# Sliding-window attention on TensorE: both head groups of a query block in one pass, and two sample chains in place of four

## The chip, the cores and the metric

The kernel runs on one core of one Trainium2 chip. The metric is the device time of one execution in microseconds (us); the median of three runs is given. One further execution was taken by the hardware profiler; all lines of the profile come from it. Engines are named as the profile names them: PE is TensorE's matmuls, PEld its weight loads, DVE is VectorE, ACT is ScalarE, POOL is GpSimd, SP the queue that issues DMAs.

## The reference

A two-layer decoder step for 512 prompt tokens and 64 sample tokens (8 sequences of 8) that share the weights. Layer 0 is a Conformer convolution (width 31) beside sliding-window attention, layer 1 a Mamba-2 mixer; each layer ends with a convolutional feed-forward network. The part that the change touches is the attention of layer 0:

```python
def sink_attention(q, k, v, q_pos, k_pos, sinks):
    b, n, tq, h, d = q.shape            # d = 64
    kv = k.shape[3]                     # 2 key/value heads
    g = h // kv                         # 4 query heads on each
    qg = q.reshape(b, n, tq, kv, g, d)
    s = jnp.einsum('bnqkgd,bnskd->bnkgqs', qg, k).astype(jnp.float32) * (d ** -0.5)
    ...                                 # window mask of 128 keys, a learned sink in each head's softmax
    o = jnp.einsum('bnkgqs,bnskd->bnqkgd', p, v)
```

The prompt's 512 queries are four blocks of 128; a block sees its own 128 keys and the 128 before it (block 0 only its own). The samples see a cache of 128 keys for each sequence, and their own 8. Everything is fp32.

## The kernel before

Activations lie with channels on the 128 partitions and the 576 tokens along the free dimension. A dense product (`mm3`, L152) takes each weight and each activation as a sum of a high and a low part and issues three matmuls (L158 to L160), 288 tokens wide; `wh` (ACT, L148) and `wl` (DVE, L149) are the parts of a weight tile. `units` runs one projection tile after another, `out_proj` an output projection.

`mix0` is layer 0's mixer. After the projections that need all of TensorE come, from L509 on, three kinds of work that are put between each other:

- The last two value projections of the convolution branch, `val_unit(1)` and `val_unit(3)`: 48 dense matmuls each.
- The depthwise convolution. Three of its four channel tiles are done by DVE, one tap an instruction (`ca`, L683). The fourth (tile 1) is done by PE: `pe_conv(k0, k1)` issues, for each tap, three matmuls of 512 columns with a diagonal matrix (`dg`, L524 to L526) and a narrow one (`df`, L529). ACT makes the diagonals, three instructions a tap (L522, L522, L528). `dg` has four buffers, two taps' worth.
- The attention. The query tiles `qf[j]` hold head j of the first key/value head on partitions 0 to 63 and head j + 4 on partitions 64 to 127; `kf` holds the two key heads in the same way. `kv` (0 or 1) is the head group. `scores(n, kv)` issues four matmuls for query block n, each with the 64 rows of its group (`sc`, L581; 256 columns wide, 128 for block 0), and calls `softmax`: on DVE a masked maximum for each head (L555), three tiny operations (L557 to L559), on ACT an exponential for each head (L562), on DVE two tiny operations and a scaling for each head (L563 to L566). `values(n, kv)` issues, for each 128-key chunk, four transposes into a bank (`pt`, L598), a copy by ACT (`ptb`, L600), and one matmul of 512 columns into the 64 partitions of its group in `po` (L602). After both groups ACT copies `po` to `of`, four instructions (L608).

The loop at L612 is a pipeline of eight steps: `scores` of a step, then filler (a value projection in the first two, five or six convolution taps after), then `values` of the step before. The score tiles `sc` (two heads a tile) take turns in three PSUM banks, `pt` in two, `po` has one.

The samples' attention (L634 to L658) is four chains, one for each half of the sequences (bh) and head group (kv): four small score matmuls in 32-column strips (`sc<-kct`, L640), one against the new keys (L642), a `softmax` of one tile, two transposes (L647, L648), two copies (L650, L651), then one matmul for the new values (L653) and four for the cached ones (L655).

Then come the high and low parts of the attention's output (`oh`, `ol`, L168 and L169), the mean over channels for the LayerNorm of the convolution (`pm`, L691, needs all four `ca`), the squares (`csq`) and the output projection of the attention (`out_proj` at L701, the first L158 that reads `oh`).

A scheduler places the instructions of each engine's queue. It keeps the results' dependences but not the order of the source; within its queue an engine issues in order.

Of the kernel before, what the change touches and what calls it, by code (L numbers as in the profile page):

```python
# [8 lines left out]
AF = mybir.ActivationFunctionType  # L9
# [3 lines left out]
P = 128  # L13
NP = 512
# [34 lines left out]
class Builder:  # L49
# [300 lines left out]
    def mix0(self):  # L350
        nc, d = self.nc, self.d
# [193 lines left out]
        def softmax(scores, masks, scl, sinks, nsinks, width):  # L545

            n = len(scores)
            mx, den = self.Z("mx", 4, bufs=4), self.Z("den", 4, bufs=4)
            neg, es = self.Z("neg", 4, bufs=4), self.Z("es", 4, bufs=4)
            sm, held = [], []  # L550
            for i, s in enumerate(scores):
                if i % 2 == 0:
                    held.append(self.S("sm", NP))
                t = held[-1][:, (i % 2) * 256:(i % 2) * 256 + width]
                nc.vector.tensor_tensor_reduce(t, s, masks, 1.0, -3.0e38, op0=ADD, op1=MAX, accum_out=mx[:, i:i + 1])  # L555
                sm.append(t)
            nc.vector.scalar_tensor_tensor(neg[:, :n], mx[:, :n], -1.0, scl, op0=MUL, op1=MUL)  # L557
            nc.vector.tensor_tensor(neg[:, :n], neg[:, :n], nsinks, op=MIN)
            nc.vector.tensor_tensor(es[:, :n], neg[:, :n], sinks, op=ADD)  # L559
            nc.scalar.activation(es[:, :n], es[:, :n], AF.Exp)  # L560
            for i, t in enumerate(sm):
                nc.scalar.activation(t, t, AF.Exp, bias=neg[:, i:i + 1], scale=scl[:, i:i + 1], accum_out=den[:, i:i + 1])  # L562
            nc.vector.tensor_tensor(den[:, :n], den[:, :n], es[:, :n], op=ADD)  # L563
            nc.vector.reciprocal(den[:, :n], den[:, :n])
            for i, t in enumerate(sm):
                nc.vector.tensor_scalar(t, t, den[:, i:i + 1], None, op0=MUL)  # L566
            return sm, held


        pos = {}  # L570

        def scores(n, kv):
            rows = slice(kv * 64, kv * 64 + 64)
            k0 = max(n - 1, 0) * P
            width = (n + 1) * P - k0
            sc = []
            for j in range(4):
                if j % 2 == 0:
                    p = self.ps("sc", "sc")
                o = p[:, (j % 2) * width:(j % 2 + 1) * width]  # L580
                nc.tensor.matmul(o, qf[j][rows, n * P:(n + 1) * P], kf[rows, k0:k0 + width], start=True, stop=True)  # L581
                sc.append(o)
            c0 = n * 8 + kv * 4
            return softmax(sc, self.cv("amask", 256 - width, width), rsq[:, c0:c0 + 4],
                           self.pv("sink_p", kv * 4, 4), nsink[:, kv * 4:kv * 4 + 4], width)

        def values(n, kv, probs):
            pr, held = probs
            rows = slice(kv * 64, kv * 64 + 64)
            if kv == 0:  # L590
                pos[n] = self.ps("po", "po")
            po = pos[n]
            k0 = max(n - 1, 0)
            nch = n + 1 - k0
            for c in range(nch):
                pt = self.ps("pt", "pt")
                for j in range(4):
                    nc.tensor.transpose(pt[:, j * P:(j + 1) * P], pr[j][:, c * P:(c + 1) * P], self.ident)  # L598
# [3 lines left out]
                nc.tensor.matmul(po[rows, :], vt[:, ch * P + kv * 64:ch * P + kv * 64 + 64], ptb,  # L602
                                 start=c == 0, stop=c == nch - 1)
                self.free(ptb)
            self.free(held)
            if kv == 1:
                for j in range(4):
                    nc.scalar.activation(of[j][:, n * P:(n + 1) * P], po[:, j * P:(j + 1) * P], AF.Copy)  # L608

        todo = [(n, kv) for n in range(4) for kv in range(2)]  # L610
# [12 lines left out]
        (n, kv), pr = ready.pop(0)  # L623
        values(n, kv, pr)

        kct = [self.S("kct", 512) for _ in range(2)]
        vc = [self.S("vc", 512) for _ in range(2)]
        for i in range(2):
# [2 lines left out]
            nc.sync.dma_start(d["wk_old"][i], kct[i].rearrange("p (b s) -> p b s", s=P)[:, :, 8:])  # L631
            nc.sync.dma_start(d["wv_old"][i], vc[i][8:, :])
        po = self.ps("po", "po")
        for bh in range(2):  # L634
            for kv in range(2):
                rows = slice(kv * 64, kv * 64 + 64)
                p = self.ps("sc", "sc")
                for b4 in range(4):
                    b = bh * 4 + b4
                    nc.tensor.matmul(p[b4 * 32:b4 * 32 + 32, 0:P], qs[rows, b * 32:b * 32 + 32],  # L640
                                     kct[bh][rows, b4 * P:(b4 + 1) * P], start=True, stop=True)
                nc.tensor.matmul(p[:, P:192], qs[rows, bh * P:(bh + 1) * P], kf[rows, NP:], start=True, stop=True)  # L642
                c0 = 32 + bh * 2 + kv
                (pr,), held = softmax([p[:, 0:192]], self.cv("smask", bh * 192, 192), rsq[:, c0:c0 + 1],
                              self.pv("sink_s", kv), nsink[:, 8 + kv:9 + kv], 192)
                pt = self.ps("pt", "pt")
                nc.tensor.transpose(pt[:, 0:P], pr[:, 0:P], self.ident)  # L647
                nc.tensor.transpose(pt[0:64, P:2 * P], pr[:, P:192], self.ident)  # L648
                ptb = self.S("ptb", NP)
                nc.scalar.activation(ptb[:, 0:P], pt[:, 0:P], AF.Copy)  # L650
                nc.scalar.activation(ptb[0:64, P:2 * P], pt[0:64, P:2 * P], AF.Copy)  # L651
                o = po[rows, bh * P:(bh + 1) * P]
                nc.tensor.matmul(o, vts[0:64, kv * 64:kv * 64 + 64], ptb[0:64, P:2 * P], start=True, stop=False)  # L653
                for b4 in range(4):
                    nc.tensor.matmul(o[:, b4 * 32:b4 * 32 + 32],  # L655
                                     vc[bh][:, b4 * P + kv * 64:b4 * P + kv * 64 + 64],
                                     ptb[:, b4 * 32:b4 * 32 + 32], start=False, stop=b4 == 3)
                self.free(held, ptb)  # L658
# [608 lines left out]
```

## Time and profile before

| | us |
|---|---|
| median of 3 runs | 1622.1 (1620.45 to 1622.54) |
| the profiled execution | 1617.26 |
| its span in the profile | 1615.5 |
| PE busy in the span | 1588.7 (98%) |
| first score matmul, from the span's start | 100.98 |
| first matmul of the attention's output projection | 196.31 |

The page divides the span into busy times, 40 slices and groups of instructions. A timeline row gives the start, how long the row lasts, the engine, the line, what it writes and reads, the array's rows and columns in use, the shape and the number of instructions; in square brackets, how long the engine had been idle before it and who released it. An fp32 matmul is recorded as two instructions, a transpose as one. Rows of pipelined matmuls overlap, so what a stretch takes is read from the start of its row to the start of the next.

### The profile page before, as it was taken

The page shows a single profiled execution, that of the slowest core. Times are in us where ns is not written, and L with a number is a line of the kernel's source. Part 1 is how long each engine was busy: PE and PEld are TensorE (multiplying, and loading weights), DVE is VectorE, ACT ScalarE, POOL GpSimd, SP SyncE. Part 2 cuts the span into 40 slices and gives each one's busy share as a digit, 9 for nine tenths or more (in the row PEclk, how much of TensorE's full clock was granted, in tenths as well). Part 3 has the DMA queues.
Part 4 walks back from the last instruction along what each step waited for, and adds up shares of the span by engine and source line. Part 5 has one row for each costly group of instructions (what it writes and reads, how often), then busy time and mean ns, then how long its engine had stood idle before and what let it go on. Part 6 is the DMA issues. An engine that isn't in the chain of part 4 may idle for free.

```text
span 1615.5 us, 28735 instructions
## 1 busy us (share of the span) xinstructions
PE 1588.7 (98%) x11704; PEld 1504.8 (93%) x11704; DVE 1026.3 (64%) x1847; ACT 696.5 (43%) x1333; POOL 109.4 (7%) x322
## 2 busy tenths in 40 slices
PE   8999999999999999999999999999899999999999
PEld 8996699999999999998997998998799999999999
DVE  7898677654365355578796676676776653554552
ACT  7248654322122122378766556557352221221220
POOL 0000001000000000010301101101110000000000
PEclk9999999999999999999999999999899999999999
DMA  7222022222222222224335325234222222222222
GB/s 229 71 73 69 1 66 90 80 91 79 80 90 70 93 87 76 83 72 141 132 82 166 102 70 176 92 97 156 97 69 89 91 80 79 92 71 87 92 80 76
DMA packets 63633, 150.05 MB, mean 93 GB/s; under 512 B 18558, under 2 KB 19582, under 8 KB 63502
## 3 DMA queue, kind: packets, MB, share of 16 engines
q1 hardware_dynamic: 63502, 148.23, 28.8%
q8 instruction: 92, 1.51, 0.4%
q14 instruction: 39, 0.32, 0.1%
HBM read 133.86 MB, written 14.34 MB: 92 GB/s over the span
## 4 chain that ended last, share of the span: by engine, by line
PE 89%; DVE 5%; ACT 4%; DMA 2%; issue 1%; POOL 0%; SPq 0%; DVEq 0%; ACTq 0%
PE mm L158 25%; PE mm L160 25%; PE mm L159 25%; DVE cconv L734 1%; DMA acb<-acd 1%; PE yp L974 1%; ACT wh L148 1%; PE pst L923 1%; PE po L602 1%; PE sc L581 1%; PE pt L180 1%; PE pyo L987 1%; PE yp L972 1%; PE mm L524 1%; PE pr L191 1%
## 5 line engine op out<-in xcount | busy, mean ns | idle before, releaser
L158 PE MATMUL mm<-hh,wh 128*128 128x288 f32 (+1 forms) x2288 | 680.6, 298 | 8.4 <-ACT wh L148 7.7
L160 PE MATMUL mm<-hh,wl 128*128 128x288 f32 x2288 | 679.8, 297 | 0.1
L159 PE MATMUL mm<-hl,wh 128*128 128x288 f32 (+1 forms) x2288 | 677.9, 297 | 0.0
L148 ACT ACTIVATE wh<-wr 128x1024 fp32r<-128x1024 f32 (+1 forms) x215 | 223.4, 1039 | 544.1 <-issue 283.3
L158 PEld LDWEIGHTS mm<-hh,wh 128*128 128x128 f32 (+1 forms) x2288 | 429.6, 188 | 14.8 <-ACT wh L148 8.0
L160 PEld LDWEIGHTS mm<-hh,wl 128*128 128x128 f32 x2288 | 429.7, 188 | 4.6 <-issue 2.8
L159 PEld LDWEIGHTS mm<-hl,wh 128*128 128x128 f32 (+1 forms) x2288 | 429.8, 188 | 3.5 <-issue 1.4
L149 DVE TENSOR_TENSOR wl<-wr,wh 128x1024 fp32r<-128x1024 f32 (+1 forms) x215 | 257.7, 1199 | 78.3 <-ACT wh L148 78.1
L158 PE MATMUL mm<-yh,wh 128*128 128x288 f32 x960 | 286.8, 300 | 2.5 <-ACT yh L168 2.5
L159 PE MATMUL mm<-yl,wh 128*128 128x288 f32 x960 | 287.6, 300 | 0.0
L160 PE MATMUL mm<-yh,wl 128*128 128x288 f32 x960 | 286.1, 299 | 0.0
L158 PEld LDWEIGHTS mm<-yh,wh 128*128 128x128 f32 x960 | 182.1, 190 | 6.9 <-issue 3.3
L159 PEld LDWEIGHTS mm<-yl,wh 128*128 128x128 f32 x960 | 182.1, 190 | 4.4 <-issue 3.2
L160 PEld LDWEIGHTS mm<-yh,wl 128*128 128x128 f32 x960 | 181.8, 190 | 2.9 <-issue 2.8
L257 DVE TENSOR_TENSOR x<-x,mm 128x288 f32<-128x288 f32 x192 | 85.7, 451 | 154.8 <-PE mm L160 154.4
L302 DVE TENSOR_TENSOR gbuf<-mm,rs 128x224 f32<-128x224 f32 x44 | 17.2, 392 | 108.0 <-PE mm L160 108.0
L313 ACT ACTIVATE gsilu<-gconv,par 128x512 f32<-128x512 f32 x44 | 31.8, 724 | 115.1 <-DVE gconv L310 115.1
L310 DVE SCALAR_TENSOR_TENSOR gconv<-gbuf,par,gconv 128x592 f32<-128x592 f32 x88 | 73.1, 831 | 1.5
L323 DVE TENSOR_TENSOR gsilu<-mm,gsilu 128x288 f32<-128x288 f32 x88 | 40.0, 455 | 50.3 <-PE mm L160 50.3
L683 DVE SCALAR_TENSOR_TENSOR ca<-seg,par,ca 128x576 f32<-128x576 f32 x90 | 71.3, 810 | 0.3
L734 DVE SCALAR_TENSOR_TENSOR cconv<-cbuf,par,cconv 128x600 f32<-128x600 f32 x72 | 61.4, 856 | 11.6 <-ACT cconv L732 10.6
L955 ACT ACTIVATE ew<-acb,ac 128x128 f32<-128x128 f32 x128 | 41.2, 390 | 37.4 <-DMA acb<-acd 17.6
(315 smaller groups left out, 1735.0 us busy)
## 6 DMA issues: line engine op xcount, KB each, us to landing
wr<-in_w_gate SPq DMA_DIRECT2D x44, 512.0 KB, 3.3
wr<-in_w_up SPq DMA_DIRECT2D x44, 512.0 KB, 3.3
wr<-in_w_in_o SPq DMA_DIRECT2D x40, 512.0 KB, 3.4
wr<-in_w_down SPq DMA_DIRECT2D x32, 448.0 KB, 3.3
wr<-in_w_down SPq DMA_DIRECT2D x16, 512.0 KB, 3.5
acb<-acd SPq DMA_DIRECT2D x32, 256.0 KB, 3.5
h<-in_h SPq DMA_DIRECT2D x32, 256.0 KB, 2.9
out_ssm_s<-h SPq DMA_DIRECT2D x32, 256.0 KB, 2.4
```

The costliest lines, as they stand in the source:

```text
L148: nc.scalar.activation(hi[:, :n], raw[:, :n], AF.Copy)
L149: nc.vector.tensor_tensor(lo[:, :n], raw[:, :n], hi[:, :n].bitcast(F32), op=SUB)
L158: nc.tensor.matmul(out, hi[:, ws], xh[:, sl], start=i == 0, stop=False)
L159: nc.tensor.matmul(out, hi[:, ws], xl[:, sl], start=False, stop=False)
L160: nc.tensor.matmul(out, lo[:, ws], xh[:, sl], start=False, stop=i == n - 1)
L257: nc.vector.tensor_tensor(self.x[m][:, sl], self.x[m][:, sl], p[:, :HB], op=ADD)
L310: nc.vector.scalar_tensor_tensor(cv[:, :592], g[:, k:592 + k], w(k), cv[:, :592], op0=MUL, op1=ADD)
L313: nc.scalar.activation(sl[:, :NP], cv[:, :NP], AF.Silu, bias=b)
L323: nc.vector.tensor_tensor(sl[:, HALF[half]], p[:, :HB], sl[:, HALF[half]], op=MUL)
L683: nc.vector.scalar_tensor_tensor(a, sv[:, :, k:k + 8], w, a, op0=MUL, op1=ADD)
L734: nc.vector.scalar_tensor_tensor(cv[:, :600], g[:, k:600 + k], w(k), cv[:, :600], op0=MUL, op1=ADD)
L955: nc.scalar.activation(ew[:, cs], acb[:, cs], AF.Relu, bias=ac[:, o:o + 1], scale=-1.0)
```

## The change

`scores` and `values` take both head groups of a block at once, and `softmax` handles eight heads in place of four. The score matmuls are issued alternately for rows 0 to 63 and 64 to 127, each group into tiles of its own; a block now has four `sc` tiles, still in three banks. In `values`, both groups' transposes and copies come first, and the two matmuls into `po` follow each other, group 1 first; a hint keeps the second in its place. The loop has four steps, each with more taps (7 or 8), and the last taps stand before the last `values`. The samples' chains become one for each bh: both groups' scores, one `softmax` of two tiles, four transposes into one bank, two copies, and the value matmuls alternately for the two column halves. The scores of both bh now precede both value parts.

```diff
-        def scores(n, kv):
-            rows = slice(kv * 64, kv * 64 + 64)
+        def scores(n):
...
-            sc = []
+            sc = [None] * 8
             for j in range(4):
                 if j % 2 == 0:
-                    p = self.ps("sc", "sc")
-                o = p[:, (j % 2) * width:(j % 2 + 1) * width]
-                nc.tensor.matmul(o, qf[j][rows, n * P:(n + 1) * P], kf[rows, k0:k0 + width], start=True, stop=True)
-                sc.append(o)
...
+                    p = [self.ps("sc", "sc") for _ in range(2)]
+                for kv in range(2):
+                    rows = slice(kv * 64, kv * 64 + 64)
+                    o = sc[kv * 4 + j] = p[kv][:, (j % 2) * width:(j % 2 + 1) * width]
+                    nc.tensor.matmul(o, qf[j][rows, n * P:(n + 1) * P], kf[rows, k0:k0 + width], start=True, stop=True)
+            return softmax(sc, self.cv("amask", 256 - width, width), rsq[:, n * 8:n * 8 + 8],
+                           self.pv("sink_p", 0, 8), nsink[:, 0:8], width, (0, 1, 4, 5, 2, 3, 6, 7))
...
             for c in range(nch):
-                pt = self.ps("pt", "pt")
-                for j in range(4):
-                    nc.tensor.transpose(pt[:, j * P:(j + 1) * P], pr[j][:, c * P:(c + 1) * P], self.ident)
-                ptb = self.S("ptb", NP)
-                nc.scalar.activation(ptb, pt, AF.Copy)
+                ptb = []
+                for kv in range(2):
+                    pt = self.ps("pt", "pt")
+                    for j in range(4):
+                        nc.tensor.transpose(pt[:, j * P:(j + 1) * P], pr[kv * 4 + j][:, c * P:(c + 1) * P], self.ident)
+                    ptb.append(self.S("ptb", NP))
+                    nc.scalar.activation(ptb[-1], pt, AF.Copy)
                 ch = k0 + c
-                nc.tensor.matmul(po[rows, :], vt[:, ch * P + kv * 64:ch * P + kv * 64 + 64], ptb,
-                                 start=c == 0, stop=c == nch - 1)
+                for kv in (1, 0):
+                    m = nc.tensor.matmul(po[kv * 64:kv * 64 + 64, :], vt[:, ch * P + kv * 64:ch * P + kv * 64 + 64], ptb[kv],
+                                         start=c == 0, stop=c == nch - 1)
+                    if kv == 0:
+                        self.tc.keep_in_program_order(m)
...
-        for t_, it in enumerate(todo):
-            ready.append((it, scores(*it)))
-            if t_ in (0, 1):
-                self.units([val_unit((1, 3)[t_])], 1)
-                if t_:
-                    self.norm_end()
+        for n in range(4):
+            ready.append((n, scores(n)))
+            if n == 0:
+                self.units([val_unit(1), val_unit(3)], 1)
+                self.norm_end()
             else:
-                pe_conv((t_ - 2) * 31 // 6, (t_ - 1) * 31 // 6)
+                pe_conv((n - 1) * 31 // 4, n * 31 // 4)
             if len(ready) > 1:
-                (n, kv), pr = ready.pop(0)
-                values(n, kv, pr)
-        (n, kv), pr = ready.pop(0)
-        values(n, kv, pr)
+                values(*ready.pop(0))
+        pe_conv(3 * 31 // 4, 31)
+        values(*ready.pop(0))
...
+            for b4 in range(4):
+                for kv in range(2):
+                    nc.tensor.matmul(po[kv * 64:kv * 64 + 64, bh * P + b4 * 32:bh * P + b4 * 32 + 32],
                                      vc[bh][:, b4 * P + kv * 64:b4 * P + kv * 64 + 64],
-                                     ptb[:, b4 * 32:b4 * 32 + 32], start=False, stop=b4 == 3)
...
+                                     ptb[:, kv * P + b4 * 32:kv * P + b4 * 32 + 32], start=False, stop=b4 == 3)
```

Where the scheduler puts this is seen at three places. In the names the number tells one tile from another.

PE, block 1's scores, before: `sc_1312` and `sc_1315` are group 0's tiles, `po_1303` the values of block 0; group 1's tiles of block 1 (`sc_1406`, `sc_1409`) come some twenty rows later.

```order
L581 MATMUL sc_1312<-kf_217,qf_212 128x256
L581 MATMUL sc_1312<-kf_217,qf_213 128x256
L581 MATMUL sc_1315<-kf_217,qf_214 128x256
L602 MATMUL po_1303<-ptb_1309,vt_222 64x512
L581 MATMUL sc_1315<-kf_217,qf_215 128x256
L524 MATMUL mm_1342<-cph_203,dg_1344 128x512
```

And with the change: `sc_1293` and `sc_1299` are group 0's tiles, `sc_1294` and `sc_1300` group 1's.

```order
L581 MATMUL sc_1293<-kf_217,qf_212 128x256
L581 MATMUL sc_1294<-kf_217,qf_212 128x256
L581 MATMUL sc_1293<-kf_217,qf_213 128x256
L581 MATMUL sc_1294<-kf_217,qf_213 128x256
L581 MATMUL sc_1299<-kf_217,qf_214 128x256
L581 MATMUL sc_1299<-kf_217,qf_215 128x256
L581 MATMUL sc_1300<-kf_217,qf_214 128x256
L581 MATMUL sc_1300<-kf_217,qf_215 128x256
L524 MATMUL mm_1343<-cph_203,dg_1345 128x512
```

The first four alternate between the groups, the last four do not: the fourth tile, `sc_1300`, takes the bank of the first, `sc_1293`, after DVE has read it. Block 2 stands in the same way; in block 3 one score matmul stands alone some twenty rows ahead of the other seven.

PE, the values of block 0, before: the matmul of group 0 (from `ptb_1309`) is in the first piece above, that of group 1 (from `ptb_1399`) follows some thirty rows later, between two score matmuls of block 2.

```order
L526 MATMUL mm_1342<-cph_203,dg_1386 128x512
L529 MATMUL mm_1343<-cas_201,df_1391 128x64
L581 MATMUL sc_1503<-kf_217,qf_212 128x256
L602 MATMUL po_1303<-ptb_1399,vt_222 64x512
L581 MATMUL sc_1503<-kf_217,qf_213 128x256
L524 MATMUL mm_1342<-cph_203,dg_1436 128x512
```

And with the change, where all seven pairs (block 0 has one chunk, the others two) stand like this one:

```order
L596 MATMUL pt_1567<-ident_73,sm_1310 128x128
L601 MATMUL po_1415<-ptb_1428,vt_222 64x512
L601 MATMUL po_1415<-ptb_1421,vt_222 64x512
L524 MATMUL mm_1343<-cph_203,dg_1486 128x512
L525 MATMUL mm_1343<-cpl_204,dg_1486 128x512
```

The two halves of `po` now stand next to each other.

ACT, around the last block's exponentials, with the change (`sm_1619` to `sm_1622` are block 3's tiles, `of` is block 1's output, `dg_1653` the first diagonal of the eight taps that follow):

```order
L598 ACTIVATE ptb_1588<-pt_1583 128x512
L560 ACTIVATE sm_1619,den_1616<-sm_1619,neg_1617,rsq_211 128x256
L598 ACTIVATE ptb_1595<-pt_1590 128x512
L560 ACTIVATE sm_1620,den_1616<-sm_1620,neg_1617,rsq_211 128x256 x2
L608 ACTIVATE of_1112<-po_1566 128x128
L608 ACTIVATE of_1113<-po_1566 128x128
L608 ACTIVATE of_1114<-po_1566 128x128
L608 ACTIVATE of_1115<-po_1566 128x128
L560 ACTIVATE sm_1621,den_1616<-sm_1621,neg_1617,rsq_211 128x256 x2
L560 ACTIVATE sm_1622,den_1616<-sm_1622,neg_1617,rsq_211 128x256 x2
L522 ACTIVATE dg_1653<-ident_73,cwh_205 128x128
```

Before, no run of exponentials has more than the four of one group, and the one ahead of the last six taps reads so (two copies, one exponential, four copies of `po`, three exponentials, then diagonals):

```order
L600 ACTIVATE ptb<-pt 128x512 x2
L560 ACTIVATE es<-es 128x4
L562 ACTIVATE sm,den<-sm,neg,rsq 128x256
L608 ACTIVATE of<-po 128x128 x4
L562 ACTIVATE sm,den<-sm,neg,rsq 128x256 x3
L522 ACTIVATE dg<-ident,cwh 128x128
```

What moved is that a diagonal now waits for up to eight exponentials ahead of it in ACT's queue. On SP one load of an output weight (`wr`) moves behind the loads of the sample caches; the rest of its order is the same but for the places of two cache loads and copies.

More of the change, by code (lines that the diff above doesn't have):

```diff
@@ L543, in mix0, with softmax @@
         of = [self.S("of") for _ in range(4)]
-        def softmax(scores, masks, scl, sinks, nsinks, width):
+        def softmax(scores, masks, scl, sinks, nsinks, width, order):
             n = len(scores)
[L548 to L556, printed above, removed]
+            mx, den = self.Z("mx", 8, bufs=4), self.Z("den", 8, bufs=4)
+            neg, es = self.Z("neg", 8, bufs=4), self.Z("es", 8, bufs=4)
+            held = [self.S("sm", NP) for _ in range(n // 2)]
+            sm = [held[i // 2][:, (i % 2) * 256:(i % 2) * 256 + width] for i in range(n)]
+            for i in order:
+                nc.vector.tensor_tensor_reduce(sm[i], scores[i], masks, 1.0, -3.0e38, op0=ADD, op1=MAX,
+                                               accum_out=mx[:, i:i + 1])
             nc.vector.scalar_tensor_tensor(neg[:, :n], mx[:, :n], -1.0, scl, op0=MUL, op1=MUL)
@@ L633, in mix0 @@
         po = self.ps("po", "po")
+        probs = []
         for bh in range(2):
+            p = [self.ps("sc", "sc") for _ in range(2)]
+            for b4 in range(4):
+                b = bh * 4 + b4
+                for kv in range(2):
+                    rows = slice(kv * 64, kv * 64 + 64)
+                    nc.tensor.matmul(p[kv][b4 * 32:b4 * 32 + 32, 0:P], qs[rows, b * 32:b * 32 + 32],
+                                     kct[bh][rows, b4 * P:(b4 + 1) * P], start=True, stop=True)
             for kv in range(2):
@@ L636, in mix0 @@
                 rows = slice(kv * 64, kv * 64 + 64)
[L637 to L655, printed above, removed]
+                nc.tensor.matmul(p[kv][:, P:192], qs[rows, bh * P:(bh + 1) * P], kf[rows, NP:], start=True, stop=True)
+            c0 = 32 + bh * 2
@@ new lines, in mix0 @@
+            probs.append(softmax([p[kv][:, 0:192] for kv in range(2)], self.cv("smask", bh * 192, 192), rsq[:, c0:c0 + 2],
+                                 self.pv("sink_s", 0, 2), nsink[:, 8:10], 192, (0, 1)))
+        for bh, (pr, held) in enumerate(probs):
+            pt = self.ps("pt", "pt")
+            for kv in range(2):
+                nc.tensor.transpose(pt[:, kv * P:(kv + 1) * P], pr[kv][:, 0:P], self.ident)
+            for kv in range(2):
+                nc.tensor.transpose(pt[0:64, (2 + kv) * P:(3 + kv) * P], pr[kv][:, P:192], self.ident)
+            ptb = self.S("ptb", NP)
+            nc.scalar.activation(ptb[0:64, 2 * P:], pt[0:64, 2 * P:], AF.Copy)
+            nc.scalar.activation(ptb[:, 0:2 * P], pt[:, 0:2 * P], AF.Copy)
+            for kv in range(2):
+                nc.tensor.matmul(po[kv * 64:kv * 64 + 64, bh * P:(bh + 1) * P], vts[0:64, kv * 64:kv * 64 + 64],
+                                 ptb[0:64, (2 + kv) * P:(3 + kv) * P], start=True, stop=False)
+            for b4 in range(4):
+                for kv in range(2):
+                    nc.tensor.matmul(po[kv * 64:kv * 64 + 64, bh * P + b4 * 32:bh * P + b4 * 32 + 32],
```

18 lines of the change are left out of this document (5 added, 13 removed).

## The prediction

> **What bounds the kernel now.** First the page: span, busy time of PE, and the chain that ended last.
>
> ```profile
> span 1615.5 us, 28735 instructions
> PE 1588.7 (98%) x11704; PEld 1504.8 (93%) x11704; DVE 1026.3 (64%) x1847; ACT 696.5 (43%) x1333; POOL 109.4 (7%) x322
> PE 89%; DVE 5%; ACT 4%; DMA 2%; issue 1%; POOL 0%; SPq 0%; DVEq 0%; ACTq 0%
> ```
>
> PE carries the kernel, so what PE is spared in the changed stretch shortens the run, as long as no other engine takes its place there. The stretch runs from the first score matmul (101 us) to the attention's output projection (196 us). The window view cuts it into five; the columns are length, then busy time of PE, PEld, DVE, ACT and POOL with instruction counts, granted clock, DMA share and GB/s.
>
> ```profile
> 100.50:119.60 19.10, 19.10 (x131) 16.97 (x129) 17.60 (x62) 12.94 (x28) 0.00 (x0) 1.00 0.23 64
> 119.60:172.40 52.80, 52.79 (x272) 35.14 (x271) 42.47 (x143) 41.72 (x141) 0.00 (x0) 1.00 0.18 55
> 172.40:174.60 2.20, 0.01 (x1) 0.02 (x1) 0.32 (x3) 2.20 (x9) 0.00 (x0) 0.98 0.00 0
> 174.60:178.00 3.40, 3.40 (x11) 2.82 (x11) 3.37 (x11) 2.78 (x10) 0.00 (x0) 0.51 0.00 0
> 178.00:197.80 19.80, 18.80 (x110) 11.82 (x109) 10.50 (x28) 13.17 (x48) 0.00 (x0) 1.00 0.00 1
> ```
>
> PE never rests from 100.5 to 172.4. Then it waits 2.2 us, and for the 3.4 us after it the clock is 0.51. From 119.6 on ACT is busy for 41.72 + 2.20 + 2.78 + 13.17 = 59.9 of 78.2 us and DVE for 42.47 + 0.32 + 3.37 + 10.50 = 56.7. So both have room, but not much: a stretch shorter by more than 18 us would hit ACT.
>
> **The score matmuls.** The timeline of PE; a stretch lasts from its start to the next row's.
>
> ```profile
> 125.00 1.99 PE L581 MATMUL sc<-kf,qf 64*128 64x256 f32 x8
> 126.92 0.49 PE L526 MATMUL mm<-cph,dg 128*128 128x512 f32 x1
> ...
> 127.51 0.70 PE L581 MATMUL sc<-kf,qf 64*128 64x256 f32 x2
> 128.14 1.07 PE L602 MATMUL po<-ptb,vt 128*64 128x512 f32 x2
> 129.14 0.70 PE L581 MATMUL sc<-kf,qf 64*128 64x256 f32 x2
> ...
> 133.28 1.57 PE L581 MATMUL sc<-kf,qf 64*128 64x256 f32 x10
> 134.78 0.44 PE L529 MATMUL mm<-cas,df 128*128 128x64 f32 x2
> ...
> 149.84 2.00 PE L581 MATMUL sc<-kf,qf 64*128 64x256 f32 x12
> 151.84 0.40 PE L640 MATMUL sc<-kct,qss 64*32 64x128 f32 x2
> ```
>
> Two instructions are one matmul. Four of one group take 1.92 us, a lone one 0.63: 0.43 each, and 0.2 for a stretch. The five at 133.28 are two of group 0 and then three of group 1 (another block's), and take 1.50 = 3 × 0.43 + 0.2: row halves do run side by side, as the longer half alone. The six at 149.84 (two and four) take 2.00, about four. That is the trace's own evidence for the first half of the change, and it also shows that part of the gain is there already.
>
> Before: 24 wide matmuls (x48 in the group below) in ten stretches are 24 × 0.43 + 10 × 0.2 = 12.3, less the 4 × 0.43 that run beside others in the two mixed stretches: 10.6 us. After: a block's first four matmuls alternate, 2 × 0.43. Then come two of group 0, and the last two of group 1 wait until DVE has read the block's first tile, since four tiles share three banks. If they come too late to pair, a block takes 6 × 0.43 + 0.2 = 2.8; if DVE is in time, 4 × 0.43 + 0.2 = 1.9. DVE's reading of the tile's two heads starts behind a 0.8 us convolution tap as often as not, so I take 2.8, three times, and 0.2 for block 3's extra stretch: 8.6. Saved 2.0, at best 4.2; if DVE is late by a tap or two in each block (0.8 to 1.6 us) the saving is gone. Block 0's narrow matmuls pair in one place of three; I count nothing for them.
>
> **The value matmuls.** Groups of PE from 100.5 to 197.9 (count | busy, mean ns | idle before), the timeline of a pair, and two stretches of layer 1, where two column halves of one bank (`yp`) are already written alternately.
>
> ```profile
> L602 PE MATMUL po<-ptb,vt 128*64 128x512 f32 x28 | 14.4, 612 | 0.0
> L581 PE MATMUL sc<-kf,qf 64*128 64x256 f32 x48 | 11.3, 402 | 0.0
> ...
> 137.62 1.93 PE L602 MATMUL po<-ptb,vt 128*64 128x512 f32 x4
> 139.49 1.09 PE L598 MATMUL pt<-ident,sm 128*128 128x128 f32 x8
> 140.51 0.70 PE L581 MATMUL sc<-kf,qf 64*128 64x256 f32 x2
> ...
> 762.18 0.66 PE L974 MATMUL yp<-ew,xdt 128*64 128x128 f32 x8
> 762.66 0.39 PE L972 MATMUL yp<-acb,hst 128*64 128x128 f32 x4
> ```
>
> One matmul into `po` takes 1.00 us (128.14 to 129.14), two of one half 1.87. Eight full-width transposes of 128 columns take 1.02; eight `yp` instructions of the same 128 columns, in two halves, take 0.48: column halves run side by side too. Before: 14 matmuls, three stretches of two and eight alone, 3 × 1.87 + 8 × 1.00 = 13.6. After: seven pairs at 1.00 = 7.0 if they overlap, 7 × 1.87 = 13.1 if they do not. The first is what `yp` shows, on another width but the same halves. Saved 6.6, at worst 0.5.
>
> **The samples' values.** One chain of four:
>
> ```profile
> 189.11 0.65 PE L655 MATMUL po<-ptb,vc 128*64 128x32 f32 x8
> 189.70 0.43 PE L653 MATMUL po<-ptb,vts 64*64 64x128 f32 x2
> 190.06 0.65 PE L655 MATMUL po<-ptb,vc 128*64 128x32 f32 x8
> ```
>
> 0.59 + 0.36 = 0.95 a chain, 3.8 for four; the column halves now alternate, so 1.9 saved (0 if what limits these 32-column matmuls is their issue, not the array). The transposes keep their number. Six `softmax` calls in place of twelve spare 30 tiny DVE and 6 tiny ACT operations, which lie beside PE: nothing. The load of one output weight moves on SP behind the cache loads; the DMA share is 0.00 from 172.4 on, so the queue is empty long before it is used: nothing. The cache loads wait for slots that block 0's transposes free, around 125 us, some ten before the samples' scores: nothing.
>
> **The stall.** ACT's rows that end in it, and PE's row that waits:
>
> ```profile
> 171.73 0.79 ACT L608 ACTIVATE of<-po 128x128 f32<-128x128 f32 x4 [2.51 <-PE po L602]
> 172.38 0.62 ACT L562 ACTIVATE sm<-sm,neg,rsq 128x256 f32<-128x256 f32 x1
> ...
> 174.13 0.40 ACT L522 ACTIVATE dg<-ident,cwh 128x128 fp32r<-128x128 f32 x1
> ...
> 174.59 0.80 PE L524 MATMUL mm<-cph,dg 128*128 128x512 f32 x1 [2.19 <-ACT dg L522]
> ```
>
> ACT stands 2.51 us before the copies of `po`, then copies (0.65), does three exponentials (1.75, so 0.58 each) and only then makes the diagonal that PE needs, 0.46 later. With the change the same chain stands in block 3 with four exponentials behind the copies: 0.65 + 2.33 + 0.46 = 3.44 after the pair into `po`, against which PE has a block of transposes (0.55) and one matmul pair of the LayerNorm mean (0.54): a wait of 2.4, as now within 0.2. The half clock after it costs half of 3.40, 1.7 us, before and after. [...]
>
> Elsewhere the new queue has these waits: eight exponentials in a row (4.7 us) for block 1 and for block 2, with PE holding 1.9 us of taps ready (two taps) and, in the queue, eight transposes, eight score matmuls or the samples' scores (1.0 and 2.8): the rest is 4.7 − 1.9 − 1.0 − 2.8, below zero. I allow 0.5 in all. At the end PE waits for the LayerNorm mean and for `ol`, DVE for PE:
>
> ```profile
> L562 ACT ACTIVATE sm<-sm,neg,rsq 128x256 f32<-128x256 f32 x24 | 14.2, 598 | 0.1
> L555 DVE CUSTOM_DVE_ANT_0 sm<-sc,cst 128x256 f32<-128x256 f32 x22 | 8.7, 420 | 7.1 <-PE sc L581 7.1
> 191.60 1.55 DVE L693 TENSOR_TENSOR ca<-ca,pm 128x288 f32<-128x288 f32 x4 [3.67 <-PE pm L691]
> ...
> 196.31 0.83 PE L158 MATMUL mm<-oh,wh 128*128 128x288 f32 x4
> 197.83 0.40 PE L159 MATMUL mm<-ol,wh 128*128 128x288 f32 x1 [0.69 <-DVE ol L169]
> ```
>
> DVE had its convolutions done 3.67 us before PE gave it the mean, and stood 7.1 us waiting for scores before that. So it can come about 10.8 us sooner, which is as much as PE asks of it: late next is DVE's last tap or the evacuation of the convolution that PE does. I allow another 0.5 there, and gain back the 0.69, since the narrower tail lets `ol` come before PE is through the means: these cancel within 0.5.
>
> **The sum.** 2.0 + 6.6 + 1.9 = 10.5 saved, 0.3 of waits added: 10.2. With the profiled execution at 1617.26 (1.8 around the span), 1607.1. That execution was 4.8 below the median; on the median, 1622.1 − 10.2 = 1611.9, and I say 1611.5, since fewer stretches also mean fewer entries that I have not counted (block 0, the samples' transposes).
>
> **Rivals.** *ACT sets the pace.* ACT has 59.9 us of work in what would be 68, in strict order, and each exponential that stands before a diagonal holds PE. For it: two of PE's waits there are on ACT already, and the runs of exponentials double. Against: 18 us of idle ACT, most of it in waits for PE (the 2.51 above). One more stall of 2.4 with its half clock costs 4.1: 1616; two, 1620. Chance 0.20, three quarters of it below 1618.9.
>
> *The halves do not overlap in `po`.* For it: 512-column pairs into one bank stand nowhere in this trace. Against: `yp`, which differs in width alone. 6.1 less: 1618. Chance 0.05. And *nothing overlaps that did not before* (the pairs are there in the queue, yet the banks' waits and the pairs' second reads keep them apart): 10.5 less is no change, 1622. Chance 0.04.
>
> *Slower.* The mechanism is the same wait, in every block: a run of eight exponentials, 4.7 us, longer than what PE has queued, so that the clock falls to half each time. At 4.1 a place the third one more than eats the gain (12.3 against 10.2); with four places it is 1628. It needs PE's queue to lack the transposes and scores that the order shows. Chance 0.06.
>
> [...] Chance 0.10.
>
> **Numbers.** The forecast proper, 1609 to 1615, has 0.55. The range from 1606.5 to 1619 takes in the better case, one more ACT stall and the unpaired `po`; it leaves out the slower case and no change, and part of two ACT stalls. Faster by more than 0.2% (3.2 us, about what a measurement can tell): 0.55 + 0.10 + 0.15 + 0.05 = 0.85. Within 0.2%: 0.05 + 0.04 = 0.09. Slower: 0.06.
>
> **What would show it.** In the changed profile the score stretches should be x16, about 2.8 us, with alternating starts in the first half; each `po` pair x4 in 1.0; the samples' value part half as long; one PE wait of about 2.4 on `dg` near 150, with a clock of about 0.5 after it; and the first matmul that reads `oh` near 186. The prediction is wrong if ACT's diagonals release PE in several long waits, if a `po` pair still takes 1.9, or if the mean (`pm`) waits for a DVE tap by more than a microsecond.

## The result and the profile after

The median went from 1622.1 to 1610.06 us (five executions of each, the ratio 0.9921, interval 0.9896 to 0.9946). A second set on another occasion gave 1620.66 and 1607.73 (0.9923, 0.9902 to 0.9944). The forecast was 1611.5. The executions with the change spread more widely than before, 1602.4 to 1613.3; the profiled one, 1613.28, is the slowest of its five, while the profiled one of before (1617.26) was below all five of its own. So the two profiles differ by 4.0 where the medians differ by 12.0, and the traces have to be compared by stage. The first lines of the page after:

```profile
span 1611.5 us, 28699 instructions
PE 1580.2 (98%) x11704; PEld 1502.4 (93%) x11704; DVE 1024.4 (64%) x1817; ACT 696.1 (43%) x1323; POOL 110.3 (7%) x322
```

PE's matmuls are as many as before and it is busy for 8.5 us less. The stage is read from the first score matmul to the first matmul that reads `oh`; in what follows that is *the stretch*. It was 196.31 − 100.98 = 95.3 and is 187.70 − 100.91 = 86.8, from this row of PE's timeline:

```profile
187.70 0.51 PE L158 MATMUL mm<-oh,wh 128*128 128x288 f32 x1
```

PE's score stretches and pairs, from the timeline after. What a stretch takes is again the start of its row to the start of the next one shown with it:

```profile
116.16 3.23 PE L581 MATMUL sc<-kf,qf 64*128 64x256 f32 x16
119.31 0.50 PE L524 MATMUL mm<-cph,dg 128*128 128x512 f32 x1
...
124.52 3.13 PE L581 MATMUL sc<-kf,qf 64*128 64x256 f32 x16
127.58 0.51 PE L526 MATMUL mm<-cph,dg 128*128 128x512 f32 x1
...
135.19 2.71 PE L581 MATMUL sc<-kf,qf 64*128 64x256 f32 x14
137.83 0.42 PE L638 MATMUL sc<-kct,qss 64*32 64x128 f32 x8
...
150.16 1.08 PE L601 MATMUL po<-ptb,vt 128*64 128x512 f32 x4
151.18 1.09 PE L596 MATMUL pt<-ident,sm 128*128 128x128 f32 x8
...
183.59 0.44 PE L656 MATMUL po<-ptb,vts 64*64 64x128 f32 x4
183.96 0.66 PE L660 MATMUL po<-ptb,vc 128*64 128x32 f32 x16
184.54 0.44 PE L656 MATMUL po<-ptb,vts 64*64 64x128 f32 x4
```

A pair into `po` now takes 1.02 (150.16 to 151.18) where two of one half took 1.87; both groups of a bh take 0.95 for the samples' values (183.59 to 184.54), as one group did. So column halves do run side by side, at 512 columns and at 32. A wide block's eight scores take 3.1. The windows of PE around what went wrong (length, then busy time of PE, PEld, DVE, ACT, POOL, granted clock, DMA share and GB/s):

```profile
136.82:140.23 3.41, 3.28 (x26) 1.98 (x27) 2.74 (x17) 3.41 (x14) 0.00 (x0) 1.00 0.01 2
140.23:147.06 6.83, 6.83 (x20) 5.26 (x21) 4.71 (x13) 4.00 (x12) 0.00 (x0) 0.50 0.00 0
147.06:153.89 6.83, 6.83 (x48) 4.00 (x46) 2.62 (x9) 4.70 (x14) 0.00 (x0) 1.00 0.17 38
153.89:157.30 3.41, 1.44 (x8) 0.72 (x6) 3.41 (x11) 3.26 (x13) 0.00 (x0) 1.00 0.29 77
157.30:160.71 3.41, 3.23 (x9) 2.66 (x10) 3.41 (x12) 2.79 (x10) 0.00 (x0) 0.50 0.48 154
```

PE waits in the fourth, and the fifth runs at half clock: that was forecast. The second was not: 6.83 us at half clock, behind a window in which PE hardly waited at all. It costs 3.4 us.

Taken apart by what PE did, each matmul counted from its start to the next one's start, without idle time and without what the half clock added (worked out from the timelines; us in the stretch):

| PE's time in the stretch | before | after | forecast of the difference |
|---|---|---|---|
| values, `po` (28) | 13.61 | 7.07 | −6.6 |
| scores, `sc<-kf,qf` (64) | 13.03 | 11.27 | −2.0 |
| samples' values (40) | 3.77 | 1.91 | −1.9 |
| taps (155) | 30.41 | 29.49 | none |
| all else | 30.28 | 29.47 | none, 0.4 in all for entries |
| PE's own work | 91.1 | 79.2 | −10.5 |
| idle | 2.55 | 2.46 | +0.3 |
| added by half clock | 1.71 | 5.12 | 0 |
| the stretch | 95.3 | 86.8 | −10.2 |

The rest of the program, in the same order in both, took 1419.2 before and 1423.8 after. PE's idle time in it accounts for that: 14.1 against 18.7. It is no effect of the change: over the fourteen profiles of this study, with the same instructions there, that part took 1414.9 to 1424.6, and the buffers-only variant of the kernel before (below) has 17.5 us idle there.

### The profile page after: what moved, and what is told of

Same layout as the page of the kernel before. It is cut to its first block, busy times and chain, and to the rows that moved or that the text cites. A ratio compares the mean times of both kernels' runs of the same rounds, so it can differ in the third digit from the quotient of the medians.

```text
span 1611.5 us, 28699 instructions
## 1 busy us (share of the span) xinstructions
PE 1580.2 (98%) x11704; PEld 1502.4 (93%) x11704; DVE 1024.4 (64%) x1817; ACT 696.1 (43%) x1323; POOL 110.3 (7%) x322
## 4 chain that ended last, share of the span: by engine, by line
PE 88%; DVE 5%; ACT 4%; DMA 3%; issue 1%; POOL 0%; SPq 0%; ACTq 0%; DVEq 0%; POOLq 0%
PE mm L158 26%; PE mm L160 25%; PE mm L159 25%; DMA acb<-acd 2%; PE yp L979 1%; DVE cconv L739 1%; PE pst L928 1%; PE pt L180 1%; ACT wh L148 1%; PE yp L977 1%; PE mm L524 1%; PE pyo L992 1%; PE pr L191 1%; PE pt L915 1%; PE mm L526 1%
## 5 line engine op out<-in xcount | busy, mean ns | idle before, releaser
L257 DVE TENSOR_TENSOR x<-x,mm 128x288 f32<-128x288 f32 x192 | 85.7, 452 | 155.7 <-PE mm L160 155.4
L739 DVE SCALAR_TENSOR_TENSOR cconv<-cbuf,par,cconv 128x600 f32<-128x600 f32 x72 | 61.5, 857 | 11.4 <-ACT cconv L737 10.3
```

Source lines behind the costliest of these rows:

```text
L257: nc.vector.tensor_tensor(self.x[m][:, sl], self.x[m][:, sl], p[:, :HB], op=ADD)
L739: nc.vector.scalar_tensor_tensor(cv[:, :600], g[:, k:600 + k], w(k), cv[:, :600], op0=MUL, op1=ADD)
```

## The experiments

The first four ask whether it is the pairs that pay, or the new order. Theory A is that the array's halves overlap and PE's time goes down by what they save; rival B that the order did it.

**No pairs in `po`.**

```diff
-    m = nc.tensor.matmul(po[kv * 64:kv * 64 + 64, :], vt[:, ch * P + kv * 64:ch * P + kv * 64 + 64], ptb[kv], ...)
+    m = nc.tensor.matmul(po, vt[:, ch * P:ch * P + P], ptb[kv], ...)
```

> Both matmuls of a pair into po use all 128 columns of the array (each with the keys' values of both groups as weights, so po holds a sum of both groups): as many instructions of the same 512 columns, but they cannot run side by side. All else as in the changed kernel. I read the stretch from the first score matmul to the first matmul that reads oh: 95.3 us before, 86.8 with the change. Theory A (the halves of the array overlap): each of seven pairs goes from 1.01 back to 1.87, so the stretch is about 6.0 longer, 92.8, and the time some 6 over the changed kernel's, 1616; within 3.4 either way if the stretch of half clock near 140 us goes or comes. Rival B (the gain is the new order with its fewer stretches and waits): the pair costs PE nothing that it did not cost before, the stretch stays within 1.5 of 86.8 and the time near 1610.

Measured: 1607.12 (before beside it 1619.84; ratio 0.992, 0.9902 to 0.9937), not slower than the changed kernel, and the stretch is 84.1, against 86.8. Theory A's sum fell, but not for rival B's reason. The pairs are slower as expected (1.72 and 1.82 below), PE's own work is 83.6 in place of 79.2; idle time and half clock, 7.6 us with the change, are 0.5. PE's timeline, then ACT's, both of this kernel:

```profile
147.93 1.88 PE L601 MATMUL po<-ptb,vt 128*128 128x512 f32 x4
149.65 1.04 PE L596 MATMUL pt<-ident,sm 128*128 128x128 f32 x8
...
151.33 1.99 PE L601 MATMUL po<-ptb,vt 128*128 128x512 f32 x4
153.15 0.60 PE L596 MATMUL pt<-ident,sm 128*128 128x128 f32 x4
```

```profile
152.61 0.59 ACT L560 ACTIVATE sm<-sm,neg,rsq 128x256 f32<-128x256 f32 x1
...
153.35 0.79 ACT L608 ACTIVATE of<-po 128x128 f32<-128x128 f32 x4
154.00 0.42 ACT L522 ACTIVATE dg<-ident,cwh 128x128 fp32r<-128x128 f32 x1
```

And ACT's and PE's rows at the same place with the change:

```profile
154.04 0.79 ACT L608 ACTIVATE of<-po 128x128 f32<-128x128 f32 x4 [0.41 <-PE po L601]
154.69 0.62 ACT L560 ACTIVATE sm<-sm,neg,rsq 128x256 f32<-128x256 f32 x1
...
156.44 0.60 ACT L560 ACTIVATE sm<-sm,neg,rsq 128x256 f32<-128x256 f32 x1
...
157.02 0.40 ACT L522 ACTIVATE dg<-ident,cwh 128x128 fp32r<-128x128 f32 x1
...
157.47 0.80 PE L524 MATMUL mm<-cph,dg 128*128 128x512 f32 x1 [2.07 <-ACT dg L522]
```

With the slow pair all of block 3's exponentials are done before `po` is ready; the scheduler puts the copies behind them, and the diagonal follows directly. With the fast pair `po` is ready four exponentials earlier, the copies go first, and the four exponentials (154.69 to 157.02, 2.33) stand between them and the diagonal. ACT's work is the same; PE waits for it idle in place of computing. The samples' score matmuls also lie otherwise between the taps, so this kernel does not tell the half clock near 140 from the wait.

**No pairs in the scores.**

```diff
-    nc.tensor.matmul(o, qf[j][rows, n * P:(n + 1) * P], kf[rows, k0:k0 + width], start=True, stop=True)
+    nc.tensor.matmul(o, qf[j][:, n * P:(n + 1) * P], kf[:, k0:k0 + width], start=True, stop=True)
```

> The score matmuls of the prompt contract over all 128 rows (both groups summed, so the scores are not those of one head): same count and width, but no two run side by side. Theory A: the changed kernel saved 2 x 0.43 in each of the three wide blocks and gave back 0.26 to 0.39 in each while PE waited for the score bank; without the pairs 2.6 is lost and about 1.0 of waiting goes, +1.6. [...] Together the stretch is 85.0 and the time some 2 under the changed kernel's. Rival D (the clock fell because of PE's short gaps between the samples' matmuls): the half clock near 140 stays and the stretch is 88.4.

Measured: 1604.95 (1619.84; 0.9913, 0.9892 to 0.9933), a stretch of 84.6. Of the two figures expected, 85.0 counts the half clock near 140 as gone with the full rows (3.4 less), a guess of mine that no run had shown, and 88.4 has it stay. That the result lies so near 85.0 is luck. The scores took 11.56 in place of 11.27, so their pairing is worth 0.3 and not 1.6: no weight load of theirs waits for a bank any more, and the 24 wide ones took 9.9, under 24 × 0.43 = 10.3, so nothing like the entry of 0.2 us a stretch is left. The half clock near 140 is gone, with PE's order the same, which is 3.4 less; the wait for the diagonal stands, and here its half clock lasts 6.83 us in place of 3.41, which is 1.7 more:

```profile
136.15:139.56 3.41, 3.41 (x30) 2.21 (x28) 2.96 (x17) 3.41 (x13) 0.00 (x0) 1.00 0.01 2
139.56:142.97 3.41, 3.41 (x19) 2.70 (x20) 3.41 (x12) 2.69 (x10) 0.00 (x0) 1.00 0.00 0
...
149.80:153.21 3.41, 1.79 (x10) 0.72 (x6) 3.41 (x11) 3.00 (x13) 0.00 (x0) 1.00 0.27 72
153.22:160.05 6.83, 6.32 (x18) 5.27 (x19) 6.83 (x17) 5.09 (x17) 0.00 (x0) 0.50 0.23 77
```

That the full rows ended the half clock near 140 is not shown by this one execution, since the unedited kernel was without it too when it was run again (below).

**Four sample chains.** The code of L634 to L658 before put back; all else as changed.

```diff
-            for b4 in range(4):
-                for kv in range(2):
-                    nc.tensor.matmul(po[kv * 64:kv * 64 + 64, ...], vc[bh][...], ptb[...], ...)
+        for bh in range(2):
+            for kv in range(2):
+                ...
+                for b4 in range(4):
+                    nc.tensor.matmul(o[:, b4 * 32:b4 * 32 + 32], vc[bh][...], ptb[...], ...)
```

> The samples' attention as four chains (one for each half of the sequences and head group) as before the change; all else as in the changed kernel. Theory A: each chain's values take 0.95 alone, four 3.8 in place of 1.9, and none of it is hidden, so the stretch is 1.9 longer, 88.7. Rival B: 30 more tiny DVE operations and 6 tiny ACT ones stand beside PE and the order is the same, so under 0.5 longer, 87.2.

Measured: 1611.81 (1619.84; 0.9947, 0.9927 to 0.9966), a stretch of 89.0 (88.7 expected). Theory A holds here by the stretch; the times by themselves (0.9947 here, 0.9921 with the change) are too close to tell. Each chain takes 0.94 by itself, and the same stretches of half clock and the same wait (2.02) stand in both:

```profile
183.36 0.43 PE L650 MATMUL po<-ptb,vts 64*64 64x128 f32 x2
183.72 0.65 PE L652 MATMUL po<-ptb,vc 128*64 128x32 f32 x8
184.30 0.43 PE L650 MATMUL po<-ptb,vts 64*64 64x128 f32 x2
```

**The order alone**: the three edits together.

> All three at once: value matmuls over all 128 columns, score matmuls over all 128 rows, samples in four chains; what is left of the change is the order. Theory A: 6.0 + 1.6 + 1.9 = 9.5 longer than the changed kernel, a stretch of 96.3, or 92.9 if the half clock near 140 goes with the full rows; time 1616 to 1620, next to nothing under before. Rival B: a stretch of at most 89 and a time within 3 of the changed kernel's 1610.

Measured: 1609.48 (1619.84; 0.9931, 0.9911 to 0.9952), a stretch of 86.1: neither half of the array runs beside the other, and the time is that of the changed kernel. PE's own work is 85.9, 6.6 more than with the change, and it has no half clock there and 0.2 idle. The window of the stretch shows it (length, PE busy, and a granted clock of 1.00):

```profile
100.89:186.97 86.08, 85.85 (x512) 68.30 (x511) 71.56 (x222) 70.01 (x224) 0.00 (x0) 1.00 0.16 48
```

Against the kernel before, 5.2 of PE's work is gone without any pair (the values are 2.2 cheaper, the scores 1.5), and so are 2.3 of waiting and 1.7 of half clock. So the kernel as changed has the gain of the pairs in PE's work, and in its first profile loses as much to ACT's wait and to the clock; in its second (below, a stretch of 83.8) it loses about two thirds. The scheduler moved other instructions too when it was given this kernel, so "the order alone" is the order as it came out.

If that is so (theory A from here on), lifting the wait must give the pairs their worth. The next three change what ACT does, the fourth only fills PE's wait.

**Six diagonal buffers.**

```diff
-    dg.append(self.segp.tile([P, P], F32R, tag="dg", bufs=4, name="dg"))
+    dg.append(self.segp.tile([P, P], F32R, tag="dg", bufs=6, name="dg"))
...
-    df = self.segp.tile([P, P], F32, tag="df", bufs=2, name="df")
+    df = self.segp.tile([P, P], F32, tag="df", bufs=3, name="df")
```

> Six buffers for the diagonals dg and three for df (four and two before): ACT may be three taps ahead of PE in place of two. By the runs so far PE's own work in the stretch of the changed kernel is 79.2 us, its idle time 2.5 and the half clock costs 5.1. [...] Rival E (ACT's work as a whole is the bound there): the wait comes back at a later tap and the stretch stays at 86 or more.

Measured: 1601.58 (1621.63; 0.9882, 0.9867 to 0.9897), a stretch of 81.0, where rival E has 86 or more. PE's own work is 79.4 (79.2 with four buffers); the wait is 0.87, and there is no half clock in the stretch (the mean granted clock of the whole span is 1.0):

```profile
151.70 0.75 PE L696 MATMUL pm<-ca,o 128*128 128x288 f32 x2 [0.56 <-DVE mx L553]
...
153.32 0.49 PE L524 MATMUL mm<-cph,dg 128*128 128x512 f32 x1 [0.87 <-ACT dg L522]
```

The scheduler also put some of PE's rows into another order here, those near 140 among them, so the buffers and that order are not told apart.

**Block 3's exponentials split around two taps**, and the same with six buffers.

```diff
             for i, t in enumerate(sm):
+                if i == 4 and between:
+                    pe_conv(*between)
...
+        plan = {3: (17, 19)}
         for n in range(4):
-            ready.append((n, scores(n)))
+            a, b = plan.get(n, (0, 0))
+            if a:
+                pe_conv((n - 1) * 31 // 4, a)
+            ready.append((n, scores(n, (a, b) if b else None)))
...
-                pe_conv((n - 1) * 31 // 4, n * 31 // 4)
+                pe_conv(b or (n - 1) * 31 // 4, n * 31 // 4)
```

> The order on ACT alone: taps 15 and 16 are traced ahead of block 3's scores and taps 17 and 18 between its fourth and fifth exponential, so that no eight exponentials stand ahead of the first diagonals that PE needs. Theory A: the wait of 2.1 falls under 0.6 and the half clock behind it (1.7) goes, 3.2 to 3.4 in all: a stretch of 83.5; the half clock near 140 stays (the order there is the same) and the time is about 3 under the changed kernel's. Rival E (ACT's work as a whole is the bound): the wait moves to another tap, 86 or more.

> Both of the two before: six diagonal buffers and block 3's exponentials split around two taps. Theory A: no wait over 0.5 for a diagonal is left, no half clock behind it; with the half clock near 140 a stretch of 83, without it 79.5, and a time of 1600 to 1606. Rival E: 86 or more.

Measured: 1603.69 (1621.63; 0.9893, 0.9876 to 0.9909), a stretch of 83.4, and with the buffers 1604.36 (0.99, 0.9883 to 0.9917) and 80.8. The first has the stretch that theory A expected, but not for its reason: the half clock near 140 is missing in this execution, and the wait is not gone. It is 1.86 at 157.68, at the third diagonal in place of the first, with its half clock (1.7) behind it. ACT's rows show why; the last four exponentials now stand there:

```profile
154.60 0.40 ACT L528 ACTIVATE df<-ident,par 128x128 f32<-128x128 f32 x1
154.89 0.60 ACT L562 ACTIVATE sm<-sm,neg,rsq 128x256 f32<-128x256 f32 x1
...
157.23 0.40 ACT L522 ACTIVATE dg<-ident,cwh 128x128 fp32r<-128x128 f32 x1
```

So on the wait rival E was right: ACT works from 148.9 on without a pause, and another order moves the wait without ending it. With the buffers, by which ACT is further ahead when that run begins, the wait is 0.8, more than the 0.5 that theory A allowed, and the stretch is 80.8 where it had 79.5. Buffers without the split gave 81.0, so the split adds next to nothing to them.

**Six useless matmuls in PE's wait.**

```diff
+            if n == 1:
+                fill = self.ps("pt", "pt")
+                for _ in range(6):
+                    self.tc.keep_in_program_order(
+                        nc.tensor.matmul(fill, cph[0][:, 0:P], cph[0][:, 0:NP], start=True, stop=True))
```

> The changed kernel with six more matmuls of 128 x 128 x 512 behind the second pair of block 1's values, which nothing reads: 6 x 0.235 = 1.4 us more work for PE, put into its wait of 2.1 us for ACT's diagonal. [...] Rival F (the half clock follows from what runs after, or from the wait for ACT as such): the stretch stays at 86.8, or grows by up to 1.4 to 88.2.

Measured: 1602.93 (1621.63; 0.989, 0.9875 to 0.9905), a stretch of 81.9. With 1.5 us more to do PE came out 4.9 sooner in the profile: 1.7 because the granted clock stays at 1.00 behind the wait (in 152.52 to 155.93, which holds it, PE is busy for 2.87 of 3.41 us, where it was 1.44 with the change), and 3.4 because the half clock near 140 is missing in this execution, which is luck. Against rival F stands the first part alone.

```profile
150.66 1.66 PE L610 MATMUL pt<-cph 128*128 128x512 f32 x6
...
154.21 0.49 PE L524 MATMUL mm<-cph,dg 128*128 128x512 f32 x1 [0.54 <-ACT dg L522]
```

```profile
152.52:155.93 3.41, 2.87 (x17) 2.16 (x15) 3.41 (x10) 3.41 (x14) 0.00 (x0) 1.00 0.48 142
155.93:159.35 3.42, 3.42 (x20) 2.97 (x19) 3.42 (x11) 3.42 (x13) 0.00 (x0) 1.00 0.18 68
```

**The changed kernel again**, unedited, beside the three that follow.

> The changed kernel once more, beside the three others. [...] So a stretch of 81.7, 83.4, 85.1 or 86.8, and PE work within 0.3 of 79.2. Rival: the half clock belongs to the program, and the stretch is 86.8 again within 0.3.

Measured: 1607.73 (1620.66; 0.9923), a stretch of 83.8 with 79.7 of PE's own work (0.5 from the first, 0.3 allowed). The half clock near 140 is not there; the wait of 2.07 and the one behind it are. The program is the same, only the grid on which the granted clock changes lies elsewhere in it, with changes here at 156.12 and 159.53, in the first profile at 157.30 and 160.71:

```profile
135.64:139.05 3.41, 3.39 (x26) 2.04 (x24) 2.32 (x15) 3.41 (x13) 0.00 (x0) 1.00 0.01 2
139.05:142.46 3.41, 3.28 (x21) 2.31 (x21) 3.41 (x16) 3.19 (x11) 0.00 (x0) 1.00 0.00 0
...
152.71:156.12 3.41, 1.50 (x8) 1.28 (x9) 3.41 (x10) 3.41 (x13) 0.00 (x0) 1.00 0.58 172
156.12:159.53 3.41, 3.41 (x12) 2.84 (x11) 3.41 (x11) 2.75 (x9) 0.00 (x0) 0.50 0.11 43
```

**Six buffers again**, unedited.

> The kernel with six buffers for dg and three for df, beside the changed kernel on one chip: median 6 to 9 us under it, a stretch of 81.0, or 82.7 where the grid falls badly on the remaining wait of 0.9. If the earlier difference was the luck of five executions, the two are within 3 us.

Measured: 1604.31 (1620.66; 0.9899, 0.9877 to 0.9921), a stretch of 81.0 again. It is 3.4 under the changed kernel beside it, not 6 to 9, and the intervals of the two ratios overlap: by the times alone it stays open whether the buffers give the 3.4 us of this set or the 8.5 between the two earlier medians. The stretch, 81.0 twice against 86.8 and 83.8, is the firmer evidence that they help.

**Six buffers in the kernel before.**

> The kernel before the change with six buffers for dg and three for df. Theory A: it has the one wait of 2.2 and its half clock of 1.7; one tap more in hand takes 0.9 of the wait and the half clock away: a stretch of 92.7 and 2 to 3 us less time, so the buffers are worth less to it than the 8 us that they gave the changed kernel. Rival G (the six buffers give the same to both, and the pairs stay worth what they were): 7 to 9 us less.

Measured: 1619.48 (1620.66; 0.9995, 0.9982 to 1.0009), no difference; the stretch is 94.5. Rival G is out, and theory A's 2 to 3 us were not seen either, though the interval allows nearly 3. The wait for the diagonal went from 2.2 to 0.2 and its half clock with it, but a half clock came at 189.3, among the samples' small value matmuls (it cost 3.2 us in the stretch; an L691 matmul behind them took 604 ns in the mean, 425 before). So in this profile the buffers did end the wait, and the clock took most of it back; how often it does so is not shown.

**Six buffers without pairs in `po`.**

> Six and three diagonal buffers, with both matmuls of a pair into po over all 128 columns (po then holds a sum of both groups), so that they cannot run side by side. Without the buffers this made the stretch shorter (84.1 against 86.8). Theory A (the pairs' PE time was only covered by ACT's wait and by the half clock): with ACT three taps ahead the pairs are worth their PE time, 11.46 - 7.07 = 4.4: a stretch of 85.4. Rival H (something else than PE's work sets the stretch there): within 1 of 81.0.

Measured: 1606.59 (1620.66; 0.9916, 0.9897 to 0.9935), a stretch of 83.0, 2.0 longer than with the pairs and between theory A's 85.4 and rival H's 81. PE's own work is 3.2 more, and 1.2 of that is hidden in waits (0.4 idle in place of 1.6). Without the buffers the stretch was 84.1 without pairs and 86.8 or 83.8 with them, so nothing for the pairs; with the buffers it is 2.0. The scheduler placed other instructions too in this kernel, so 2.0 is a figure for the two orders as they came out.

## Why the prediction was right, and where not

- *The values*, 6.6 saved: measured 6.54. `yp` as the evidence for `po` held, at four times the width.
- *The samples' values*, 1.9: measured 1.86, and 1.9 to 2.2 when undone.
- *The scores*, 2.0: measured 1.76 in all, but only 1.3 of it for the wide blocks (10.66 before, 9.35 after; I had 8.6) and 0.4 for block 0 (2.36 and 1.93), for which I had counted nothing. The fourth tile came too late to pair, as taken, and PE's weight loads also stood still for its bank, 1.5 us in four places, which the sum left out. The best case was mis-summed besides: 3 × (4 × 0.43 + 0.2) + 0.2 is 6.0, so 4.6 saved and not 4.2. The row is that of PE's weight loads, total, times, longest:

```profile
PEld sc L581 <- DVE mx L553: 1.5, 4, 0.5
```

- *Fewer entries*, 0.4: mis-sized. Taps, transposes and the rest came out 1.7 cheaper.
- *The stall*, one wait of 2.4 on `dg` with half clock after it: 2.07, at 155.4 and not 150, and 3.41 at 0.50. The elsewhere waits (0.5 allowed) added nothing; PE's idle time is 2.46 against 2.55.
- *First matmul on `oh` near 186*: 187.7, and 184.9 in the second profile.
- *The clock*: the step that failed. I read "2.2 us of idle, then half clock" as a price on waits, and so saw only one place for it. The changed kernel had a second one without such a wait: 6.83 us at 0.50 from 140.23, behind 3.41 us (136.82 to 140.23) in which PE was busy for 3.28. What the new order has there are the samples' small score matmuls, now close together behind the prompt's score matmuls, which use 64 of the array's rows. Sixteen of their instructions lie between 137.83 and 140.09 (the first eight are shown above), which before lay between 151.84 and 158.78 with taps among them. First a row of the changed kernel, then two of the kernel before:

```profile
139.75 0.42 PE L638 MATMUL sc<-kct,qss 64*32 64x128 f32 x6
```

```profile
153.27 0.42 PE L640 MATMUL sc<-kct,qss 64*32 64x128 f32 x6
158.43 0.42 PE L640 MATMUL sc<-kct,qss 64*32 64x128 f32 x6
```

That these matmuls bring the half clock is not shown: in the second profile the same order has PE busy for 3.39 and 3.28 in the two windows from 135.64 on, and the clock stays at 1.00. The half clock cost 3.4 in one profile of the two. The saving I had not counted, 1.7, offset half of it. So the stretch came out 8.5 shorter in one profile and 11.5 in the other, where 10.2 was forecast, and that 1611.5 came so near the median is in part luck.
- *The rivals.* Against the kernel before, the forecast's mechanism held where the clock did not interfere: in the second profile PE has 11.4 us less work, the wait and its half clock are as before, and the stretch is 11.5 shorter. But the kernel in the new order without any pair has the same time within the noise (1609.5), with no wait and no half clock in its stretch. So "ACT sets the pace", 0.20, was near in one thing: part of what the pairs save ends as a wait for ACT. No further stall of 2.4 came, which was the price it had. That the terms of the sum were right says that PE's work was rightly priced, not that this work was all that bounded the stretch. "The halves do not overlap" and "nothing overlaps" are out by the 1.02 of a pair.
- *The better case* of the range, 1607.5 (0.10), took off 2.2 for the fourth score tile, which came too late, and 1.7 for a full clock behind a short wait, which no run had shown by then. In the runs half clock came behind waits of 2.07, 2.02 and 1.86 and none behind 0.87 and 0.54.

## What to carry to other kernels

Two matmuls in two halves of the array ran side by side here (1.02 for a pair into `po`, 1.87 for two in one half), and the saving on PE could be summed from single rows; whether the time follows depends on the engine that feeds the next matmul, and here one more tap of look-ahead for ACT took 2.8 to 5.8 us off the stretch, where the pairs in the scores were worth 0.3 of PE's work. Before counting a PE saving as time, look at what ACT or DVE must finish in the same stretch, and undo the saving once with the order kept as far as the scheduler lets you: if nothing gets slower, it was not PE alone that bounded. And the granted clock was 0.50 for 3.41 us behind a wait of 2.07 us, and in one profile of two for 6.83 us where PE hardly waited, so it is worth reading the granted clock of a stretch from more than one execution before a figure is put on a change.

## What the runs showed of the hardware

The windows with a granted clock of 0.50 that were read, each with the time for which PE was busy in the 3.41 us before it (us):

| profile | half clock from | lasts | PE busy in the 3.41 before |
|---|---|---|---|
| before | 174.59 | 3.41 | 1.22 |
| before | 1157.56 | 10.24 | 1.49 |
| changed, first | 140.23 | 6.83 | 3.28 |
| changed, first | 157.30 | 3.41 | 1.44 |
| changed, first | 1109.62 | 3.41 | 1.46 |
| changed, first | 1157.40 | 6.83 | 1.69 |
| changed, second | 156.12 | 3.41 | 1.50 |
| no pairs in the scores | 153.22 | 6.83 | 1.79 |

In seven of the eight PE was busy for 1.22 to 1.79 of the 3.41 us before. In the one from 140.23 it was busy for nearly all of them. The kernel with four sample chains has a half clock there too (an L525 matmul takes 0.63 from 141.21 on and 0.40 again at 147.00). What brought it is not shown: the changed kernel's second profile has 3.39 and 3.28 near there and the kernel with full-row scores 3.41 and 3.41, with a granted clock of 1.00 throughout. With the six useless matmuls 2.87 was followed by 1.00. The changed kernel has it in one profile and not in the next, so one profile without it does not show that an edit ended it.

The rest of the program has half clock too, 10.24 us of it in the profile before and 3.41 + 6.83 in the first one with the change, which is 5.1 us of time in each. Over the profiles the mean granted clock of the span is 0.994 to 1.0. That is up to 9.7 us of 1610 by my estimate, which is much of the spread between executions of one kernel.
